# Two halves of the first expert product's columns: 512-column matrix products, an accumulating DMA, a gelu in a later job

## The chip, the cores and the metric

The program runs on one core of a Trainium2 chip. The metric is the time of one execution on the device, in microseconds (us); a lower time is better. The engines are TensorE (PE in the profile; PEld is its weight load), VectorE (DVE), ScalarE (ACT), GpSimd (POOL) and SyncE (SP). Each runs its own instructions in the order in which they stand, and waits for the others on semaphores. DMAs are issued from the queues of SP, ACT and, after the change, POOL.

## The reference, cut to what matters

Two encoder layers over 256 tokens of width 1024. Each has a token-mixing part and an expert part. The change works on the first product of the expert part. The reference looks 128 rows up per token in a table of 16384 rows:

```
act = jax.nn.gelu(jnp.einsum('cd,chkd->chk', hc, u_tab[ic]))
w = (gc * act.astype(jnp.float32)).astype(hc.dtype)
return jnp.einsum('chk,chkd->cd', w, v_tab[ic])
```

`hc` are tokens, `ic` the chosen rows (8 heads of 16), `gc` their weights by softmax.

## The kernel before, in words

The kernel doesn't gather rows. It multiplies all 256 tokens by all 16384 rows of `u_tab` (128 jobs of 128 rows), takes the gelu, multiplies by a table of weights that is zero where a row wasn't chosen, and multiplies the outcome by all of `v_tab` (128 more jobs). Both layers do so.

**Numbers in two parts.** TensorE works on float32r. To keep float32's precision each operand is split into a high and a low part: `hi` is the value rounded by an ACT copy (`split_hi`, L230), `lo` is what is left, by a DVE subtraction (`split_lo`, L233). A product is then three matmuls: low weights by high tokens (L238), high weights by low tokens (L239), high weights by high tokens (L240), which `prod` adds up in one PSUM tile. The weights are the 128x128 operand that is loaded, the tokens the one that streams: 256 columns. A job of the first expert product (`u_job`, L1031) has 8 chunks of the 1024 input features, so 24 matmuls.

**A job.** The loop at the end of the program takes each job of a list through the same steps: SP loads its 512 KB of weights (`raw`, three buffers), ACT writes `whi`, DVE writes `wlo` (three buffers each, two jobs ahead of use), TensorE multiplies into one of three PSUM banks (`main`), and the job's `post` empties the bank while the next job multiplies. In a first expert job `post` is a gelu on ACT, from PSUM. What it writes depends on how far the table of weights has got (`state["tok"]` tokens): with none it writes the gelu into the big table (L1050); else the tokens whose weights are there go to a tile `gel` (L1045) and DVE multiplies them into the table (L1048), and ACT writes the others (L1047).

**Work in the background.** While the 128 first expert jobs run, the choice of the rows is made in the background, in pieces of a fixed budget a job: on DVE the top 16 of scores and candidates (its recorded line is L93), then the table of weights, 64 blocks a layer, each with one-hot tiles on DVE (L970, L973), 8 small matmuls (`gw`, L988 and L989), DVE products (L998) and ACT copies (L1002).

**Order.** The program text is not the final order. A scheduling layer works out a time for each instruction and places it on its engine's queue by that; instructions recorded as in order (`VB`, `SB`) keep theirs. What stands on each queue must so be read from the built program.

**Storage.** Tiles come from pools; a tag names a place and `bufs` how many of it there are. `hhi` and `hlo` hold the tokens' high and low parts, `cst` the constants (identity, a row of numbers, cosines and sines of the rotary step), `gB1` a place that in turn holds `raws`, the gates `mixG`, and part of the table.

Of the kernel before, what the change touches and what calls it, by code (L numbers as in the profile page):

```python
# [22 lines left out]
NC8 = 8  # L23
# [5 lines left out]
LATE = 320 + DEPTH * 384  # L29
# [87 lines left out]
def _body(tc, nc, A, pp, big, hp, st, wk, ps, dr, stop, dump):  # L117
# [14 lines left out]
    cst = pp.tile([128, C_MASK], F32, name="cst")  # L132
    ident, iota = (cst[:, o:o + 128] for o in (C_ID, C_IOTA))
    cos, sin = cst[:, C_COS:C_COS + T], cst[:, C_SIN:C_SIN + T]
# [28 lines left out]
    def late_setup():  # L163
        nc.sync.dma_start(cst, A["cst"][:, :C_MASK])
        late = state["raws"][:, NAREA * D:]
        tmp = late[:, :320]
        nc.sync.dma_start(tmp, A["cst"][:, C_MASK:])
        for t, n in ((sink, "a_sink"),):
            nc.sync.dma_start(t, bass.AP(tensor=A[n].tensor, offset=A[n].offset, ap=[[0, 128], [1, 16]]))
# [11 lines left out]
        d2 = late[:, 320 + DEPTH * 256:].rearrange("p (a d) -> p a d", d=64)  # L181
# [53 lines left out]
    def prod(out, whi, wlo, xhi, xlo, n, start=True, stop=True):  # L235

        for c in range(n):
            PE.matmul(out, wlo(c), xhi(c), start=start and c == 0, stop=False)  # L238
            PE.matmul(out, whi(c), xlo(c), start=False, stop=False)  # L239
            PE.matmul(out, whi(c), xhi(c), start=False, stop=stop and c == n - 1)  # L240
# [46 lines left out]
    def new_h():  # L287
        hi = hp.tile([128, NC8, T], F32R, name="hhi", tag="hhi")
        lo = hp.tile([128, NC8, T], F32R, name="hlo", tag="hlo")
        return hi, lo  # L290

    def stats(r, m, direct):
# [7 lines left out]
        sq = wk.tile([128, T], F32, name="sq", tag="t1k", bufs=5)  # L300
# [53 lines left out]
    def norm_to_h(r, hi, lo, sc, sh, g, b):  # L354
# [10 lines left out]
        def emit(m):  # L365
            h = wk.tile([128, T], F32, name="hf", tag="t1k", bufs=5)
            S.activation(h, r[:, m], AF.Identity, scale=fold[:, 0, 0, m:m + 1], bias=fold[:, 0, 1, m:m + 1])
            marks["hi"] = split_hi(hi[:, m], h)
            marks["lo"] = split_lo(lo[:, m], h, hi[:, m])
# [17 lines left out]
    def start_chunk(m):  # L387
# [3 lines left out]
        hi, lo = state["h"]  # L391
        x = state["x"][:, m]
        V.tensor_scalar(opsc[:, m:m + 1], mods[0][:, 8 + m:9 + m], 1.0, None, op0=OP.add)
        h = wk.tile([128, T], F32, name="hf", tag="t1k", bufs=5)
        S.activation(h, x, AF.Identity, scale=opsc[:, m:m + 1], bias=mods[0][:, m:m + 1])
        split_hi(hi[:, m], h)
        split_lo(lo[:, m], h, hi[:, m])
# [20 lines left out]
    def layer(l):  # L418
# [3 lines left out]
        def mix_begin():  # L422
            m = big.tile([128, 64, T], F32, name="mixA", tag="gA")
            state["m"] = m
            state["bh"] = (big.tile([128, 24, T], F32R, name="mixB0", tag="gB0"), big.tile([128, 8, T], F32R, name="mixB2", tag="gB2"))
            mains((0, 1, 5))
            state["ab"] = []
            mf = m.rearrange("p a b -> p (a b)")
# [15 lines left out]
        def rope_post(n, slot, scale):  # L444
            def post(out):
                dst = state["m"][:, slot]
                rot = wk.tile([128, T], F32, name="ropet", tag="t1k", bufs=5)
# [4 lines left out]
                def gen(lane):  # L452
                    yield 0.0
                    V.tensor_tensor(dst, dst, cos, op=OP.mult)
# [10 lines left out]
        def v_post(dst):  # L465
            def post(out):
                raw = wk.tile([128, T], F32, name="vx", tag="t1k", bufs=5)
# [20 lines left out]
        def bchunk(a, k):  # L488

            k = 16 * a + k  # L490
            return state["bh"][0][:, k] if k < 24 else state["bh"][1][:, k - 24]

        def bsplit(src, k):
            split_hi(bchunk(0, k), src)
            split_lo(bchunk(1, k), src, bchunk(0, k))
# [84 lines left out]
        def head_c(lane, c):  # L580
# [25 lines left out]
            def tail(lane):  # L606
# [6 lines left out]
                sq = wk.tile([128, T], F32, name="sqc", tag="t1k", bufs=5)  # L613
# [105 lines left out]
        def gates_begin():  # L719
            state["gt"] = big.tile([128, 32, T], F32, name="mixG", tag="gB1")  # L720
        jobs.append(Job(func=gates_begin))
# [20 lines left out]
        def branch_job(m, half):  # L742
            def mm(hi, lo):
                out = main_bank([128, 2, T], name="main")
                for b in range(2):
                    o = 4 * (2 * half + b)
                    prod(out[:, b], lambda c: hi[:, 4 * b + c], lambda c: lo[:, 4 * b + c],
                         lambda c: bchunk(0, o + c), lambda c: bchunk(1, o + c), 4)
                return out

            def post(out):
# [4 lines left out]
                if half:  # L756
                    V.tensor_tensor(t, t, acc0, op=OP.add)
                    acc = wk.tile([128, T], F32, name="gacc", tag="t1k", bufs=5)
                    V.tensor_tensor(acc, t[:, 0], t[:, 1], op=OP.add)
                    xh, xl = state["mx"]  # L760
                    split_hi(xh[:, m], acc, scale=0.5)
                    V.scalar_tensor_tensor(xl[:, m], acc, 0.5, xh[:, m].bitcast(F32), op0=OP.mult, op1=OP.subtract)
# [26 lines left out]
        def out_job(m):  # L789
            def mm(hi, lo):  # L790
                out = main_bank([128, T], name="main")
                xh, xl = state["mx"]
                prod(out, lambda c: hi[:, c], lambda c: lo[:, c], lambda c: xh[:, c], lambda c: xl[:, c], NC8)
# [14 lines left out]
        def ln1():  # L808
            state["h"] = new_h()
            hi, lo = state["h"]  # L810
            norm_to_h(state["r"], hi, lo, mods[l][:, 32:40], mods[l][:, 24:32],
# [199 lines left out]
        def wq_job(k):  # L1011
            def mm(hi, lo):
                out = main_bank([128, T], name="main")
                xh, xl = state["h"]
                prod(out, lambda c: hi[:, c], lambda c: lo[:, c], lambda c: xh[:, c], lambda c: xl[:, c], NC8)
                return out

            def post(out):
                q = wk.tile([128, T], F32, name="qf", tag="t1k", bufs=5)
# [11 lines left out]
        def u_job(j):  # L1031
            def mm(hi, lo):
                out = main_bank([128, T], name="main")
                xh, xl = state["h"]
                prod(out, lambda c: hi[:, c], lambda c: lo[:, c], lambda c: xh[:, c], lambda c: xl[:, c], NC8)
# [306 lines left out]
```

## Time and profile before

| | |
|---|---|
| median of 3 runs | 2375.04 us (2373.57 to 2375.71) |
| the profiled execution's own time | 2374.35 us |
| span of its trace | 2372.5 us |
| TensorE busy | 2294.8 us, 97% of the span |
| VectorE busy | 1819.4 us, 77% |
| ScalarE busy | 1262.5 us, 53% |
| GpSimd busy | 0.2 us |

The span is the time from the first to the last instruction of the trace. Busy time is the time in which an engine has at least one instruction at work; matmuls overlap one another in it, so that it does not say how fast they follow each other. The starts of neighbouring rows of the timeline say that.

### The profile page before, as it was taken

To read this page: it belongs to the slowest core of one execution; us is meant where nothing else is said; L and a number is where in the kernel's file an instruction comes from. 1 tells how busy PE (TensorE), PEld (TensorE's weight loads), DVE (VectorE), ACT (ScalarE), POOL (GpSimd) and SP (SyncE) were. 2 spreads that over 40 slices of the span, in tenths; PEclk is the share of its full clock that TensorE was granted. 3 is DMA by queue.
4 is the path that set the end of the run, shared out by engine and by line. 5 is a ranking of instruction groups with operands and counts; after the bars stand their busy time and mean duration, and the time that the engine had idled before them with its cause. 6 is when DMAs were issued, how large, how long until landed. Compare 5 with 4: busy or idle time off the path is not lost.

```text
span 2372.5 us, 43573 instructions
## 1 busy us (share of the span) xinstructions
PE 2294.8 (97%) x16488; PEld 2129.3 (90%) x16488; DVE 1819.4 (77%) x3929; ACT 1262.5 (53%) x2539; POOL 0.2 (0%) x4
## 2 busy tenths in 40 slices
PE   6999999999999999999989999999999999999997
PEld 5999898999999988888789989999999999888886
DVE  8687788998889666667677867889888895665555
ACT  4755545455554454555467554455555544555444
POOL 0000000000000000000000000000000000000000
PEclk9999999999999999999989999999999999999998
DMA  8467654554545576767544765545544455665563
GB/s 335 155 228 255 213 188 146 169 183 160 163 159 163 181 229 238 248 237 254 193 155 154 260 226 202 189 149 172 178 161 161 161 169 195 238 209 194 194 212 107
DMA packets 128033, 461.80 MB, mean 195 GB/s; under 512 B 15440, under 2 KB 20048, under 8 KB 124624
## 3 DMA queue, kind: packets, MB, share of 16 engines
q1 hardware_dynamic: 126816, 453.25, 57.0%
q10 hardware_dynamic: 1008, 5.77, 0.6%
q8 instruction: 131, 2.15, 0.4%
q14 instruction: 78, 0.64, 0.1%
HBM read 450.31 MB, written 5.24 MB: 192 GB/s over the span
## 4 chain that ended last, share of the span: by engine, by line
PE 80%; DVE 13%; DMA 4%; ACT 2%; issue 2%; SPq 0%; DVEq 0%; ACTq 0%
PE main L238 15%; PE main L239 15%; PE main L240 15%; PE vacc L1077 10%; PE vacc L1076 10%; PE vacc L1078 10%; DVE wlo L233 4%; DMA mixA<-in_w_ada 2%; DVE topk L93 2%; PE gw L988 1%; PE gw L989 1%; DVE ada L252 1%; PE ssc L873 1%; ACT whi L230 1%; DMA raw<-in_w_out 1%
## 5 line engine op out<-in xcount | busy, mean ns | idle before, releaser
L233 DVE TENSOR_TENSOR wlo<-raw,whi 128x1024 fp32r<-128x1024 f32 x723 | 878.6, 1218 | 355.1 <-ACT whi L230 353.2
L238 PE MATMUL main<-hhi,wlo 128*128 128x256 f32 x3456 | 1002.1, 290 | 10.3 <-DVE wlo L233 9.5
L240 PE MATMUL main<-hhi,whi 128*128 128x256 f32 x3456 | 979.0, 283 | 0.0
L239 PE MATMUL main<-hlo,whi 128*128 128x256 f32 x3456 | 978.9, 283 | 0.0
L230 ACT ACTIVATE whi<-raw 128x1024 fp32r<-128x1024 f32 x720 | 761.7, 1058 | 393.5 <-PE vacc L1078 323.6
L238 PEld LDWEIGHTS main<-hhi,wlo 128*128 128x128 f32 x3456 | 663.3, 192 | 18.3 <-DVE wlo L233 12.1
L239 PEld LDWEIGHTS main<-hlo,whi 128*128 128x128 f32 x3456 | 664.3, 192 | 0.6
L240 PEld LDWEIGHTS main<-hhi,whi 128*128 128x128 f32 x3456 | 663.6, 192 | 0.0
L1077 PE MATMUL vacc<-wlo,wv 128*128 128x512 f32 x1024 | 398.6, 389 | 0.0
L1076 PE MATMUL vacc<-whi,wv 128*128 128x512 f32 x1024 | 398.6, 390 | 0.0
L1078 PE MATMUL vacc<-whi,wv 128*128 128x512 f32 x1024 | 398.4, 389 | 0.0
L1076 PEld LDWEIGHTS vacc<-whi,wv 128*128 128x128 f32 x1024 | 192.1, 188 | 40.3 <-ACT whi L230 0.4
L1077 PEld LDWEIGHTS vacc<-wlo,wv 128*128 128x128 f32 x1024 | 192.2, 188 | 40.0 <-DVE wlo L233 0.5
L1078 PEld LDWEIGHTS vacc<-whi,wv 128*128 128x128 f32 x1024 | 192.2, 188 | 39.8
L1045 ACT ACTIVATE gel<-main 128x256 f32<-128x256 f32 (+20 forms) x192 | 56.6, 295 | 298.7 <-PE main L240 298.7
L973 DVE TENSOR_TENSOR oha<-ohe,ijg 128x512 f16<-128x512 f16 x256 | 98.3, 418 | 0.9
L970 DVE TENSOR_TENSOR ohe<-iota,ijg 128x1024 f16<-128x1024 f16 x128 | 87.1, 682 | 0.2
L252 DVE CUSTOM_DVE_ANT_0 mixA<-mixA,cact,prm 128x1024 f32<-128x1024 f32 x48 | 61.5, 1280 | 32.0 <-DMA mixA<-in_w_ada 32.0
L1048 DVE TENSOR_TENSOR GB<-GB,gel 128x256 f32<-128x256 f32 (+29 forms) x128 | 46.6, 364 | 46.0 <-ACT gel L1045 44.5
L238 PE MATMUL main<-mixB,wlo 128*128 128x256 f32 x256 | 73.5, 290 | 2.2 <-ACT mixB L230 2.0
L239 PE MATMUL main<-mixB,whi 128*128 128x256 f32 x256 | 72.4, 284 | 0.0
L988 PE MATMUL gw<-ohe,oha 128*128 128x128 f16 x512 | 72.3, 222 | 0.0
(228 smaller groups left out, 2229.9 us busy)
## 6 DMA issues: line engine op xcount, KB each, us to landing
raw<-in_p_u SPq DMA_DIRECT2D x256, 512.0 KB, 3.3
raw<-in_p_v SPq DMA_DIRECT2D x256, 512.0 KB, 3.4
raw<-in_w_in SPq DMA_DIRECT2D x134, 512.0 KB, 4.2
mixA<-in_w_ada SPq DMA_DIRECT2D x48, 512.0 KB, 5.3
raw<-in_w_br SPq DMA_DIRECT2D x32, 512.0 KB, 3.3
adav<-in_w_ada SPq DMA_DIRECT2D x32, 512.0 KB, 4.5
raw<-in_p_wq SPq DMA_DIRECT2D x26, 512.0 KB, 3.5
ada<-in_w_ada SPq DMA_DIRECT2D x8, 1024.0 KB, 15.8
```

Source lines behind the costliest of these rows:

```text
L230: return S.activation(hi, src, AF.Copy, scale=scale)
L233: return V.tensor_tensor(lo, src, hi.bitcast(F32), op=OP.subtract)
L238: PE.matmul(out, wlo(c), xhi(c), start=start and c == 0, stop=False)
L239: PE.matmul(out, whi(c), xlo(c), start=False, stop=False)
L240: PE.matmul(out, whi(c), xhi(c), start=False, stop=stop and c == n - 1)
L252: V.tensor_tensor_reduce(out=buf[:, k], in0=buf[:, k], in1=state["cact"], scale=1.0, scalar=prm[:, P_BADA + 48 * l + n:P_BADA + 48 * l + n ...
L970: V.tensor_tensor(flat(eq), iota16.rearrange("p (c k) -> p c k", k=2)[:, None].to_broadcast([128, 2 * NB, 64, 2]), twice(ijg[:, 0:2]), op= ...
L973: V.tensor_tensor(flat(a[:, i:i + 1]), flat(eq[:, 0:1]), ijg[:, 2 + i, :, None, :].to_broadcast([128, NB, 64, 2]), op=OP.mult)
L988: PE.matmul(p[:, k], a[:, 0, k], b[:, k], start=True, stop=False)
L1076: PE.matmul(o, wl[:, tt], hi, start=first, stop=False)
L1077: PE.matmul(o, wh[:, tt], lo, start=False, stop=False)
L1078: PE.matmul(o, wh[:, tt], hi, start=False, stop=last)
```

## The change

- The tokens' two parts lie in one tile `h`, high and low side by side for each chunk.
- In the first expert product (`prod_apart`) the high weights meet both token parts in one matmul of 512 columns; the high part's sum lands in columns 0 to 255 of the bank and the low part's in 256 to 511. The low weights meet the high tokens in one of 256 columns, added to the first half. 16 matmuls a job instead of 24, with the same 768 columns a chunk.
- The halves must then be added. ACT copies both out of PSUM (`more`, `u`), and a DMA issued from POOL adds `more` to `u` (`accum_op`). The gelu (`gated`) works on `u`; the text calls it four jobs later, and the last four are called ahead of the second product.
- All other products still use three matmuls.
- To make room: cosines and sines no longer stay in `cst`, but are loaded into the gates' tile at each layer's start; the gates' tile is taken at the layer's start too; the row of numbers goes to a temporary place; the two `adav` tiles share the place of `h`.

```diff
+    def prod_apart(out, whi, wlo, x, n):
+
+
+        for c in range(n):
+            PE.matmul(out, whi(c), x(c), start=c == 0, stop=c == n - 1, skip_group_check=True)
+            PE.matmul(out[:, 0], wlo(c), x(c)[:, 0], start=False, stop=c == n - 1, skip_group_check=True)
...
     def new_h():
-        hi = hp.tile([128, NC8, T], F32R, name="hhi", tag="hhi")
-        lo = hp.tile([128, NC8, T], F32R, name="hlo", tag="hlo")
-        return hi, lo
+        return hp.tile([128, NC8, 2, T], F32R, name="h", tag="h")
...
             state["ab"] = []
+            state["gt"] = big.tile([128, 32, T], F32, name="mixG", tag="gB1")
...
+            nc.sync.dma_start(state["gt"][:, 6:8].rearrange("p a b -> p (a b)"), A["cst"][:, C_COS:C_COS + 2 * T])
...
         def u_job(j):
             def mm(hi, lo):
-                out = main_bank([128, T], name="main")
-                xh, xl = state["h"]
-                prod(out, lambda c: hi[:, c], lambda c: lo[:, c], lambda c: xh[:, c], lambda c: xl[:, c], NC8)
+                out = main_bank([128, 2, T], name="main")
+                x = state["h"]
+                prod_apart(out, lambda c: hi[:, c], lambda c: lo[:, c], lambda c: x[:, c], NC8)
                 return out
 
             def post(out):
                 while j >= 64 and state["GB0"] is None:
                     bgs["topk"].step(0)
+                u = wk.tile([128, T], F32, name="u", tag="t1k", bufs=6)
+                more = wk.tile([128, T], F32, name="more", tag="more", bufs=4)
+                S.activation(more, out[:, 1], AF.Copy)
+                S.activation(u, out[:, 0], AF.Copy)
+                nc.gpsimd.dma_start(u, more, accum_op=OP.add)
+                added.append(lambda: gated(u))
+                if len(added) > 4:
+                    added.popleft()()
+
+            def gated(u):
                 dst = slots(j, j + 1)[0][:, 0]
                 n = state["tok"]
                 if n:
-                    t = wk.tile([128, T], F32, name="gel", tag="t1k", bufs=5)
-                    S.activation(t[:, :n], out[:, :n], AF.Gelu_apprx_tanh)
+                    S.activation(u[:, :n], u[:, :n], AF.Gelu_apprx_tanh)
                     if n < T:
-                        S.activation(dst[:, n:], out[:, n:], AF.Gelu_apprx_tanh)
-                    V.tensor_tensor(dst[:, :n], dst[:, :n], t[:, :n], op=OP.mult)
+                        S.activation(dst[:, n:], u[:, n:], AF.Gelu_apprx_tanh)
+                    V.tensor_tensor(dst[:, :n], dst[:, :n], u[:, :n], op=OP.mult)
                 else:
-                    S.activation(dst, out, AF.Gelu_apprx_tanh)
+                    S.activation(dst, u, AF.Gelu_apprx_tanh)
                 state["jc"] = j + 1
             return Job(src=A["p_u"][l, j], mm=mm, post=post)
+        added = deque()
...
         def v_begin():
+            while added:
+                added.popleft()()
             drain()
```

TensorE's queue before, at the start of the first layer's first expert jobs (`main1` and `main5` are PSUM banks; the number behind a name tells one tile from another):

```order
L239 MATMUL main1_5092<-hlo_4290,whi_4984 128x256
L240 MATMUL main1_5092<-hhi_4289,whi_4984 128x256
...
L238 MATMUL main5_5134<-hhi_4289,wlo_5032 128x256
L239 MATMUL main5_5134<-hlo_4290,whi_5031 128x256
L240 MATMUL main5_5134<-hhi_4289,whi_5031 128x256
```

The same place after:

```order
L246 MATMUL main1_5091<-h_4289,whi_4983 128x512
L247 MATMUL main1_5091<-h_4289,wlo_4984 128x256
L246 MATMUL main5_5129<-h_4289,whi_5030 128x512
L247 MATMUL main5_5129<-h_4289,wlo_5031 128x256
L246 MATMUL main5_5129<-h_4289,whi_5030 128x512
```

Three matmuls of 256 columns a chunk have become one of 512 and one of 256.

ScalarE's queue before, in the same jobs (`GA` is the big table, `whi` the high weights of a job three further on):

```order
L1050 ACTIVATE GA_4393<-main1_5092 128x256
L230 ACTIVATE whi_5118<-raw_4998 128x1024
L1050 ACTIVATE GA_4393<-main5_5134 128x256
L230 ACTIVATE whi_5160<-raw_5045 128x1024
L1050 ACTIVATE GA_4393<-main0_5176 128x256
```

ScalarE's queue after, a few jobs on; between `L1048` of a tile `u` and `L1063` of the same number, POOL's DMA adds to that tile:

```order
L1047 ACTIVATE more_5516<-main0_5498 128x256
L1048 ACTIVATE u_5515<-main0_5498 128x256
L1063 ACTIVATE GA_4392<-u_5476 128x256
L230 ACTIVATE whi_5552<-raw_5457 128x1024
L1047 ACTIVATE more_5547<-main1_5529 128x256
L1048 ACTIVATE u_5546<-main1_5529 128x256
L1063 ACTIVATE GA_4392<-u_5515 128x256
L230 ACTIVATE whi_5591<-raw_5496 128x1024
L1047 ACTIVATE more_5586<-main5_5568 128x256
L1048 ACTIVATE u_5585<-main5_5568 128x256
L1063 ACTIVATE GA_4392<-u_5546 128x256
```

The gelu of a job (`u_5515`) stands behind the copies of the next job (`u_5546`), ahead of the next `whi`: one job later, not four. The scheduling layer has moved it up. The whole queue was read: the distance is one job for 248 of the 256 jobs, two or three for three jobs of each layer, none for each layer's last.

SyncE's queue before, at the start of the program:

```order
L1189 DMA raw_130<-in_w_in 128x1024
L164 DMA cst_82<-in_cst 128x768
L167 DMA raws_106<-in_cst 128x320
L169 DMA sink_80<-in_a_sink 128x16
L179 DMA raws_106<-in_c_lambda 128x512
L430 DMA mixA_241<-in_d_w 128x2048
L1189 DMA raw_277<-in_w_in 128x1024
```

The same place after:

```order
L1206 DMA raw_130<-in_w_in 128x1024
L162 DMA ident_82<-in_cst 128x128
L165 DMA raws_106<-in_cst 128x320
L167 DMA raws_106<-in_cst 128x128
L169 DMA sink_80<-in_a_sink 128x16
L179 DMA raws_106<-in_c_lambda 128x512
L436 DMA mixA_241<-in_d_w 128x2048
L441 DMA mixG_244<-in_cst 128x512
L1206 DMA raw_279<-in_w_in 128x1024
```

The load of cosines and sines into `mixG` stands ahead of the seventh job's weights (`raw_277`, now `raw_279`). It writes where `raws` was, so it waits for the last reader of `raws`.

## Rows read from the trace of the kernel before

**Rows 1.** The page's head: busy us, share of span, instructions.

```profile
span 2372.5 us, 43573 instructions
...
PE 2294.8 (97%) x16488; PEld 2129.3 (90%) x16488; DVE 1819.4 (77%) x3929; ACT 1262.5 (53%) x2539; POOL 0.2 (0%) x4
```

**Rows 2.** Timeline of PE: start us, duration us, instruction; first expert product.

```profile
599.84 0.28 PE L239 MATMUL main<-hlo,whi 128*128 128x256 f32 x1
...
601.04 0.28 PE L240 MATMUL main<-hhi,whi 128*128 128x256 f32 x1
```

**Rows 3.** Timeline of PE, second expert product.

```profile
899.70 0.39 PE L1076 MATMUL vacc<-whi,wv 128*128 128x512 f32 x1
...
902.88 0.39 PE L1078 MATMUL vacc<-whi,wv 128*128 128x512 f32 x1
```

**Rows 4.** Windows in the first expert product of layer one: busy us by engine.

```profile
core 0: us, PE busy (x) PEld busy (x) DVE busy (x) ACT busy (x) POOL busy (x), PEclk, DMA share, GB/s
440.00:460.00 20.00, 20.00 (x169) 20.00 (x168) 20.00 (x88) 9.38 (x14) 0.00 (x0) 1.00 0.54 182
460.00:480.00 20.00, 20.00 (x169) 20.00 (x168) 20.00 (x99) 9.41 (x14) 0.00 (x0) 1.00 0.53 173
500.00:520.00 20.00, 20.00 (x170) 20.00 (x169) 19.65 (x24) 9.17 (x15) 0.00 (x0) 1.00 0.52 165
760.00:780.00 20.00, 20.00 (x189) 19.79 (x188) 18.70 (x47) 9.63 (x25) 0.00 (x0) 1.00 0.52 165
```

**Rows 5.** Chain of waits from 440 to 520 us: shares by line.

```profile
by line: DVE topk L93 33.9%; DVE wlo L233 20.3%; PE main L238 14.9%; PE main L239 14.5%; PE main L240 14.4%; issue 1.8%; PE ijg L941 0.4%; DVEq L233 0.0%
```

**Rows 6.** Lines L1050 and L1045: count, ns min/median/max, first and last start, forms.

```profile
L1050 ACT ACTIVATE GA<-main x64: 384/384/387, 436.1 to 1694.1; 128x256 f32<-128x256 f32 x64
```

**Rows 7.** The same view of line L1045.

```profile
L1045 ACT ACTIVATE gel<-main x192: 173/298/384, 529.0 to 2003.1; 128x256 f32<-128x256 f32 x32, 128x4 f32<-128x4 f32 x4, 128x16 f32<-128x16 f32 x4, 128x24 f32<-128x24 f32 x4
```

**Rows 8.** Timeline of ACT, first expert jobs after the table of weights is done.

```profile
817.32 0.38 ACT L1045 ACTIVATE gel<-main 128x256 f32<-128x256 f32 x1 [1.55 <-PE main L240]
817.60 1.05 ACT L230 ACTIVATE whi<-raw 128x1024 fp32r<-128x1024 f32 x1
820.20 0.38 ACT L1045 ACTIVATE gel<-main 128x256 f32<-128x256 f32 x1 [1.55 <-PE main L240]
```

**Rows 9.** Timeline of ACT, jobs beside the table of weights.

```profile
640.91 0.26 ACT L1045 ACTIVATE gel<-main 128x108 f32<-128x108 f32 x1 [1.60 <-PE main L240]
641.07 0.29 ACT L1047 ACTIVATE GB<-main 128x148 f32<-128x148 f32 x1
641.24 1.06 ACT L230 ACTIVATE whi<-raw 128x1024 fp32r<-128x1024 f32 x1
642.20 0.49 ACT L1002 ACTIVATE GB<-gw 128x84 f32<-128x84 f32 x3
...
653.93 0.27 ACT L1045 ACTIVATE gel<-main 128x120 f32<-128x120 f32 x1 [1.99 <-PE main L240]
```

**Rows 10.** The page's DMA issues: count, KB each, median us from issue to landing.

```profile
raw<-in_p_u SPq DMA_DIRECT2D x256, 512.0 KB, 3.3
...
ropet<-mixA SPq DMA_DIRECT2D x104, 32.0 KB, 3.5
...
out_x<-r SPq DMA_DIRECT2D x8, 128.0 KB, 1.9
```

**Rows 11.** Line L450, the DMAs of `ropet` inside SBUF.

```profile
DMA to landing us min/median/max: 1.8/3.5/6.9
```

**Rows 12.** Timeline of the program's start: SyncE's queue, VectorE, ScalarE.

```profile
37.73 0.33 SPq L1189 DMA_DIRECT2D raw<-in_w_in  x1
...
42.87 0.41 DVE L184 TENSOR_REDUCE lams<-raws 128x4 f32<-128x256 f32 x1
...
45.47 1.05 ACT L230 ACTIVATE whi<-raw 128x1024 fp32r<-128x1024 f32 x1
```

More of the change, by code (lines that the diff above doesn't have):

```diff
@@ L167, in late_setup @@
         nc.sync.dma_start(tmp, A["cst"][:, C_MASK:])
+        iota = late[:, LATE - 128:]
+        nc.sync.dma_start(iota, A["cst"][:, C_IOTA:C_IOTA + 128])
         for t, n in ((sink, "a_sink"),):
@@ L233, in split_lo, with prod @@
         return V.tensor_tensor(lo, src, hi.bitcast(F32), op=OP.subtract)
-    def prod(out, whi, wlo, xhi, xlo, n, start=True, stop=True):
+    def prod(out, whi, wlo, x, n):
         for c in range(n):
-            PE.matmul(out, wlo(c), xhi(c), start=start and c == 0, stop=False)
-            PE.matmul(out, whi(c), xlo(c), start=False, stop=False)
-            PE.matmul(out, whi(c), xhi(c), start=False, stop=stop and c == n - 1)
+            PE.matmul(out, wlo(c), x(c)[:, 0], start=c == 0, stop=False)
+            PE.matmul(out, whi(c), x(c)[:, 1], start=False, stop=False)
+            PE.matmul(out, whi(c), x(c)[:, 0], start=False, stop=c == n - 1)
+    def prod_apart(out, whi, wlo, x, n):
+        for c in range(n):
+            PE.matmul(out, whi(c), x(c), start=c == 0, stop=c == n - 1, skip_group_check=True)
+            PE.matmul(out[:, 0], wlo(c), x(c)[:, 0], start=False, stop=c == n - 1, skip_group_check=True)
     def ada_load(l, i, buf, k=None):
@@ L438, in mm @@
                 state["out"] = out
[L439 to L440 removed]
+                x = state["h"]
+                prod(out, lambda c: hi[:, c], lambda c: lo[:, c], lambda c: x[:, c], NC8)
                 return out
@@ L486, in vtok, with bpair @@
             return state["m"][:, slot:slot + n].rearrange("p a b -> p (a b)").rearrange("p (t e) -> p t e", t=2)
-        def bchunk(a, k):
-            k = 16 * a + k
-            return state["bh"][0][:, k] if k < 24 else state["bh"][1][:, k - 24]
+        def bpair(k):
+            return state["bh"][0][:, k] if k < 12 else state["bh"][1][:, k - 12]
         def bsplit(src, k):
-            split_hi(bchunk(0, k), src)
-            split_lo(bchunk(1, k), src, bchunk(0, k))
+            p = bpair(k)
+            split_hi(p[:, 0], src)
+            split_lo(p[:, 1], src, p[:, 0])
         def to_keys(e, lane):
@@ L791, in mm @@
                 out = main_bank([128, T], name="main")
-                xh, xl = state["mx"]
-                prod(out, lambda c: hi[:, c], lambda c: lo[:, c], lambda c: xh[:, c], lambda c: xl[:, c], NC8)
+                x = state["mx"]
+                prod(out, lambda c: hi[:, c], lambda c: lo[:, c], lambda c: x[:, c], NC8)
                 return out
@@ L1123, in vstage @@
         def vstage(i, k):
-            if k == 0:
-                state["ada", i % 2] = hp.tile([128, 2, D], F32, name="adav", tag=("hhi", "hlo")[i % 2])
+            if i == k == 0:
+                both = hp.tile([128, 2, 2, D], F32, name="adav", tag="h")
+                for n in range(2):
+                    state["ada", n] = both[:, n]
             ada_load(*todo[i], state["ada", i % 2], k)
```

66 lines of the change are left out of this document (29 added, 37 removed).

## The prediction

> **What bounds the kernel now.** I read the page's head first [rows 1]: TensorE is busy in 97% of the span, VectorE in 77%, ScalarE in 53%, GpSimd not at all. Busy overlaps, so the second view is the timeline of TensorE, where the distance of starts is what counts. In the first expert product ten distances of 256-column matmuls take 601.04 - 599.84 = 1.20 us: 120 ns each [rows 2]. In the second, fourteen distances of 512-column matmuls take 902.88 - 899.70 = 3.18 us: 227.1 ns each [rows 3]. The second is not twice the first: 256 more columns cost 107.1 ns, so a matmul has some 12.9 ns of its own besides its columns (120 - 107.1). A first expert job has 24 matmuls, 2.88 us, and the timeline of ScalarE shows jobs exactly that far apart: 820.20 - 817.32 [rows 8]. Beside the table of weights four jobs take 653.93 - 640.91 = 13.02 us, 3.255 each [rows 9], since small matmuls of that table are added. So TensorE sets the pace of these jobs, at the granted clock 1.00 [rows 4].
>
> The third view is by windows, to see who comes next: VectorE is busy in all of 440 to 480 us, in 98% of 500 to 520, and in 94% at 760 to 780 [rows 4]. In the chain of waits of 440 to 520 us VectorE holds 54% (33.9 + 20.3) and TensorE's three lines the rest [rows 5]. There both are at their limit. That stage is 80 us long, some 80 / 2.88 = 28 jobs a layer.
>
> How many jobs are of which kind: 64 take the gelu with no weights there (L1050) [rows 6]; of 192 with weights 32 have all 256 columns, so come after the table is done [rows 7]. So 64 + 32 = 96 plain jobs, and 160 beside the table, in both layers.
>
> **The change part by part.**
>
> TensorE: a chunk of 120 x 3 = 360 ns becomes 227.1 + 120 = 347.1 ns. That is 12.9 ns a chunk, 103 ns a job (8 chunks), 26.4 us in 256 jobs. The columns are the same, so only the cost per matmul is saved. A plain job would go from 2.88 to 2.777 us, one beside the table from 3.255 to 3.152. Here a rule speaks for less. The Trainium skill (TensorE: Matmul & The Clock Gate, "Back-to-back issue gap") gives an isolated matmul about 2.5 ns besides its columns; 8 matmuls fewer in 256 jobs would then be worth 5 us. The rows show five times that in this stream of changing weights.
>
> VectorE: its work stays. In the 28 jobs a layer where it is full, a shorter TensorE job only waits for `wlo` sooner: I take their gain out, 56 x 0.103 = 5.8 us. Elsewhere it has 6% or more to spare, TensorE gains 3%.
>
> PSUM: the bank of a job is filled wholly instead of by half; there are three banks still, so nothing.
>
> ScalarE: per job it gets two copies of 256 columns from PSUM. The row nearest is the gelu from PSUM: 0.38 us, the next instruction starting 0.28 after it (817.60 - 817.32) [rows 8]. 0.56 us more a job on an engine that is busy for 9.6 of 20 us [rows 4], 1.6 of each 3.2 us: it fits. What it waits for is the matter. The gelu now waits for POOL's DMA, and the built order has it one job behind, not four. Behind that gelu stand in ScalarE's queue `whi` of a job to come, then the copies of the job after. So each DMA lies on a ring: `u` of job j copied, DMA j (its time from there to the waiting gelu I call L), gelu j, `whi`, copies of job j+2, DMA j+2. One turn of it is two jobs. In plain jobs the turn takes L + 0.28 (gelu) + 0.96 (`whi`, 642.20 - 641.24 [rows 9]) + 0.28 (`more`) + 0.38 (`u` to its end) = L + 1.90. Beside the table the gelu is 0.33 (641.24 - 640.91) and the copies out of `gw` 0.49 [rows 9]: L + 2.44. TensorE's two jobs take 5.554 and 6.304. The ring is hidden while L is under 3.65 us in plain jobs and under 3.86 beside the table; `whi` and `wlo` are made two jobs ahead, which covers the shift. If that cover is gone, a job takes half a turn. All jobs together then cost 96 x ((L + 1.90)/2 - 2.88) + 160 x ((L + 2.44)/2 - 3.255) = 128 L - 511 us against before: zero at L = 3.99, and 12.8 us for each tenth more.
>
> What L is, no row shows: POOL issues nothing before. From below: a DMA of the same 128 KB on SP's queue lands 1.9 us after its issue at the quiet end of the program [rows 10]. From above: 32 KB inside SBUF lands after 1.8 to 6.9 us, median 3.5, four of them in a row and behind weight loads [rows 10, 11]. At the place itself a weight load of four times the bytes lands after 3.3 us [rows 10], with the DMA engines busy 0.48 to 0.54 [rows 4]. The bytes are those of the first row, the place that of the last. I take 3.0, with the software queue and the second read in it, which would hide it. At 1.9 nothing changes; at 6.9 the formula gives +372 us. The Trainium skill (DMA: Bandwidth & Descriptors, "Anatomy of one DMA — SWDGE (gpsimd) path") gives about 2.0 us plus the bytes at 436 GB/s for one DMA from GpSimd; estimated from that page 2.3 us, which is hidden too. No run here shows a DMA of that queue.
>
> POOL's queue holds nothing else; a DMA that waits there holds only later ones of its kind, and `more` has four buffers. The 128 KB a job add a quarter to the bytes of a weight load, so a DMA share of 0.5 becomes some 0.63, and the weight loads' 3.3 us have three buffers.
>
> End of each layer's jobs: the last gelu waits for its own DMA, with the `whi` of the second product's third job ahead of it and the fourth behind. That one is needed three jobs later; nothing is lost. Without that cover it would cost L once a layer, 6 us.
>
> Program start: the seventh job's weights were issued at 37.73 us; now cosines and sines stand ahead and wait for the last reader of `raws`, which starts at 42.87 and takes 0.41 [rows 12]. The load goes out some 6 us later, at about 43.7, and lands some 4 us on, about 48. ScalarE wanted it at 45.47 [rows 12] and waits 2 to 3 us, within the two jobs of lead. I charge 0.5 us, at most 3. In layer two the same load stands behind weights and waits for nothing late. The merged `h` and `adav`, and the smaller constants, change places only.
>
> Sum: 26.4 - 5.8 - 0.5 = 20 us less than the profiled execution's 2374.35, so 2354. The runs' median is 0.7 us above that execution. 4.7 us (0.2%) is about what a measurement can tell from no change.
>
> **The rivals.**
>
> The ring decides (slower). Place: the gelu on ScalarE waiting for POOL's DMA in every job. It speaks for it that the built order leaves one job of lead, and that transfers in a busy queue have taken 3.5 us at the median and up to 6.9 [rows 10, 11]; against it the 1.9 us of an equal transfer. From L = 3.99 on it costs; at 4.22 it is +29 us, 2404 with the start's half us, at 4.5 +65, at 5.0 +129. Chance 0.28.
>
> A special form of it: GpSimd can't write its DMA's descriptors while VectorE works, so L grows by up to one `wlo`, 1.2 us, to 4.2: 128 x 4.2 - 511 = +27, 2401. Its chance, 0.05, is inside the 0.28. The Trainium skill (SBUF — State Buffer, "Who interferes with whom") has such a lock, for VectorE's two-port modes; by it two-tensor operations such as `wlo` don't take the lock for writing. Most of VectorE's work here is of that kind.
>
> Nothing changes (within 0.2%): the own cost of a matmul belongs to the change of weights and columns in another way than two rows of unmixed widths show, so a mixed pair takes near 360 ns; or L sits at 3.95 to 4.03. Then 2370 to 2380. Chance 0.10.
>
> VectorE binds longer: if the jobs at 94% are bound as well, another 50 jobs lose their 0.103 us, 5 us: 2359. Or not at all, and the 5.8 us come back: 2348. Both are still the forecast's case, whose own range is 2346 to 2364. Chance of faster by over 0.2%: 0.62, a tenth of it from L between 3.65 and 3.95.
>
> **How the numbers follow.** Faster 0.62, same 0.10, slower 0.28. The likeliest case gives 2354. Low end: all of the 26.4 us and nothing lost would be 2348, and 4 us more for what mixing widths may give, 2344; under it 0.04. High end: of the ring's 0.28 I leave 0.15 out, above L = 4.22: 2404.
>
> **What would show it.** Right: starts of a 512-column and the next matmul 227 and 120 ns apart; plain jobs 2.78 us apart, those beside the table 3.15; TensorE's idle small; landing of `u` under 3.6 us after issue; VectorE full from 440 to 520 us. Wrong: ScalarE's idle in front of the gelu (L1058, L1063) ended by POOL's DMA and TensorE's idle in front of L246 ended by `whi` or `wlo`: the ring. If pairs stand 360 ns apart, the saving per matmul was wrong. If weight loads land much later than 3.3 us and `whi` waits for them, the added transfers cost what I took as free.

## The result and the profile after

The change makes the kernel slower: 2521.6 us median of 4 runs (2517.82 to 2526.15) against 2374.89 us of 4 runs of the kernel before (2373.57 to 2375.71), a ratio of 1.0622 with a 95% interval of 1.0605 to 1.0640. The forecast was 2354 us, its range ended at 2404. The profiled execution's span is 2520.4 us, 147.9 more than [rows 1].

The page of the kernel after: the head with each engine's busy time, the DMA queue of GpSimd (packets, MB, share of 16 engines' span), the chain that ended last by engine, the groups of the DMA and of one gelu, and two DMA issues with their median time to landing.

```profile
PE 2335.8 (93%) x14440; PEld 2026.4 (80%) x14440; DVE 1811.5 (72%) x3919; ACT 1414.6 (56%) x3071; POOL 220.6 (9%) x260
...
q0 software_dynamic: 36864, 33.57, 8.6%
...
PE 47%; issue 26%; DVE 9%; DMA 7%; POOL 7%; ACT 2%; SPq 0%; POOLq 0%; DVEq 0%; ACTq 0%
...
L1049 POOL DMA_DIRECT2D u<-more x256 | 220.4, 861 | 1933.4 <-ACT u L1048 832.6
...
L1058 ACT ACTIVATE u<-u 128x256 f32<-128x256 f32 (+20 forms) x200 | 66.7, 333 | 296.5 <-DMA u<-more 296.3
...
raw<-in_p_u SPq DMA_DIRECT2D x256, 512.0 KB, 4.2
...
u<-more POOLq DMA_DIRECT2D x256, 128.0 KB, 5.2
```

No engine has become the bound: TensorE fell from 97% [rows 1] to 93% of a longer span. What is new is idle time that a DMA ends, 296.3 us in front of the gelu at L1058, and a time to landing of 5.2 us for `u`. Weight loads, 3.3 us before [rows 10], take 4.2. The chain books 26% as "issue", waits for which it finds no releaser; the timelines say what was waited for.

The views that the forecast named for the ring (copies of a job, its DMA, its gelu, then `whi` and the copies of a later job) show it. First the timelines of ScalarE and GpSimd in plain jobs (start, duration, instruction, idle time before it and what ended it):

```profile
469.97 0.42 ACT L1063 ACTIVATE GA<-u 128x256 f32<-128x256 f32 x1 [5.07 <-DMA u<-more]
470.30 1.04 ACT L230 ACTIVATE whi<-raw 128x1024 fp32r<-128x1024 f32 x1
471.24 0.36 ACT L1047 ACTIVATE more<-main 128x256 f32<-128x256 f32 x1
471.51 0.37 ACT L1048 ACTIVATE u<-main 128x256 f32<-128x256 f32 x1
471.77 0.41 ACT L1063 ACTIVATE GA<-u 128x256 f32<-128x256 f32 x1
472.07 1.05 ACT L230 ACTIVATE whi<-raw 128x1024 fp32r<-128x1024 f32 x1
473.02 0.38 ACT L1047 ACTIVATE more<-main 128x256 f32<-128x256 f32 x1
473.29 0.39 ACT L1048 ACTIVATE u<-main 128x256 f32<-128x256 f32 x1
477.36 0.42 ACT L1063 ACTIVATE GA<-u 128x256 f32<-128x256 f32 x1 [3.68 <-DMA u<-more]
...
472.17 0.86 POOL L1049 DMA_DIRECT2D u<-more  x1 [6.12 <-ACT GA L1063]
473.97 0.86 POOL L1049 DMA_DIRECT2D u<-more  x1 [0.94 <-ACT u L1048]
```

Read one turn: the gelu starts at 469.97, `whi` and both copies follow without a gap, `u` is done at 471.51 + 0.37 = 471.88, GpSimd issues at 472.17, and the gelu that waits for this DMA starts at 477.36. So L = 477.36 - 471.88 = 5.48 us, the rest of the turn 1.91 (the forecast had 1.90), the turn 7.39, and a turn is two jobs: 3.70 us a job.

The whole stage says the same. The first rows are the first expert product of layer one in the kernel before, its first matmuls (first and last start) and the first of the second product; then the same of the kernel after:

```profile
L238 PE MATMUL main<-hhi,wlo x1024: 279/283/385, 431.0 to 834.0; 128*128 128x256 f32 x171
L1076 PE MATMUL vacc<-whi,wv x512: 387/389/478, 834.4 to 1183.1; 128*128 128x512 f32 x171
```

```profile
L246 PE MATMUL main<-h,whi x1022: 390/395/775, 429.6 to 899.9; 128*128 128x512 f32 x171
...
L1092 PE MATMUL vacc<-whi,wv x512: 387/389/794, 903.2 to 1257.5; 128*128 128x512 f32 x171
```

Before, the stage takes 834.4 - 431.0 = 403.4 us, 3.15 a job. After, 903.2 - 429.6 = 473.6, which is 3.70 a job: the half turn. That is 70.2 us more in layer one. The second product, too, goes from 348.7 us to 354.3 between its first and last start, 5.6 us. Counted in the same way, layer two has 71.0 and 5.2 us. Together 152 us; the spans differ by 148.

VectorE and TensorE now idle, and the DMA engines are busier. Before, TensorE was busy in all of the two windows that follow, VectorE for 51.30 and 56.05 us of 60, with a DMA share of 0.49 and 0.51. The same windows of after (PE, PEld, DVE, ACT, POOL busy, then the granted clock, DMA share, GB/s):

```profile
600.00:660.00 60.00, 55.15 (x370) 45.86 (x369) 41.25 (x83) 38.32 (x132) 13.50 (x16) 1.00 0.77 177
720.00:780.00 60.00, 54.07 (x348) 45.01 (x347) 44.52 (x95) 35.03 (x113) 13.76 (x16) 0.94 0.70 169
```

VectorE is at 69% and 74%. 16 DMAs in 60 us are 3.75 us a job here as well. In the second window the mean granted clock is 0.94, stretches at 2.4 GHz and some at 1.2 GHz, beside 1.00 in [rows 4]; TensorE had idled in it for 6 us.

### The profile page after: what moved, and what is told of

It is laid out like the page before. It is cut to its first block, busy times and chain, and to the rows that moved or that the text cites. A ratio compares the mean times of both kernels' runs of the same rounds, so it can differ in the third digit from the quotient of the medians.

```text
span 2520.4 us, 40768 instructions
## 1 busy us (share of the span) xinstructions
PE 2335.8 (93%) x14440; PEld 2026.4 (80%) x14440; DVE 1811.5 (72%) x3919; ACT 1414.6 (56%) x3071; POOL 220.6 (9%) x260
## 3 DMA queue, kind: packets, MB, share of 16 engines
q0 software_dynamic: 36864, 33.57, 8.6%
## 4 chain that ended last, share of the span: by engine, by line
PE 47%; issue 26%; DVE 9%; DMA 7%; POOL 7%; ACT 2%; SPq 0%; POOLq 0%; DVEq 0%; ACTq 0%
PE vacc L1093 9%; PE vacc L1092 9%; PE vacc L1094 9%; POOL u L1049 7%; PE main L238 6%; PE main L239 5%; PE main L240 5%; DMA u<-more 4%; DVE wlo L233 3%; DMA mixA<-in_w_ada 2%; ACT whi L230 1%; DVE ada L259 1%; DMA raw<-in_w_in 1%; PE main L246 1%; DMA raw<-in_w_out 1%
## 5 line engine op out<-in xcount | busy, mean ns | idle before, releaser
L246 PE MATMUL main<-h,whi 128*128 128x512 f32 x2048 | 759.5, 410 | 23.9 <-ACT u L1048 23.7
L247 PE MATMUL main<-h,wlo 128*128 128x256 f32 x2048 | 588.5, 287 | 10.7 <-DVE wlo L233 10.2
L246 PEld LDWEIGHTS main<-h,whi 128*128 128x128 f32 x2048 | 394.3, 193 | 117.9 <-ACT u L1048 33.7
L238 PE MATMUL main<-h,wlo 128*128 128x256 f32 x1408 | 410.1, 292 | 11.4 <-DVE wlo L233 11.3
L247 PEld LDWEIGHTS main<-h,wlo 128*128 128x128 f32 x2048 | 396.2, 193 | 29.8 <-DVE wlo L233 29.2
L239 PE MATMUL main<-h,whi 128*128 128x256 f32 x1408 | 397.9, 283 | 0.0
L240 PE MATMUL main<-h,whi 128*128 128x256 f32 x1408 | 397.8, 283 | 0.0
L1049 POOL DMA_DIRECT2D u<-more x256 | 220.4, 861 | 1933.4 <-ACT u L1048 832.6
L238 PEld LDWEIGHTS main<-h,wlo 128*128 128x128 f32 x1408 | 269.0, 191 | 19.7 <-DVE wlo L233 13.5
L239 PEld LDWEIGHTS main<-h,whi 128*128 128x128 f32 x1408 | 269.6, 192 | 0.6
L240 PEld LDWEIGHTS main<-h,whi 128*128 128x128 f32 x1408 | 269.4, 191 | 0.0
L1058 ACT ACTIVATE u<-u 128x256 f32<-128x256 f32 (+20 forms) x200 | 66.7, 333 | 296.5 <-DMA u<-more 296.3
L992 PE MATMUL gw<-ohe,oha 128*128 128x128 f16 x512 | 79.4, 226 | 60.2 <-DVE oha L977 50.6
L1061 DVE TENSOR_TENSOR GB<-GB,u 128x256 f32<-128x256 f32 (+26 forms) x128 | 47.2, 370 | 91.6 <-ACT u L1058 61.4
```

The source lines that it names most:

```text
L238: PE.matmul(out, wlo(c), x(c)[:, 0], start=c == 0, stop=False)
L239: PE.matmul(out, whi(c), x(c)[:, 1], start=False, stop=False)
L240: PE.matmul(out, whi(c), x(c)[:, 0], start=False, stop=c == n - 1)
L246: PE.matmul(out, whi(c), x(c), start=c == 0, stop=c == n - 1, skip_group_check=True)
L247: PE.matmul(out[:, 0], wlo(c), x(c)[:, 0], start=False, stop=c == n - 1, skip_group_check=True)
L992: PE.matmul(p[:, k], a[:, 0, k], b[:, k], start=True, stop=False)
```

## The experiments

**Theories.** *Ring*: the gelu's lead is one job, a turn takes two, and L is too long for it. *Load*: the two copies and the added 128 KB a job cost the time by themselves, and the wait is only where it shows. *Pair*: a 512-column and a 256-column matmul save nothing against three of 256. *Rest*: the moved storage and loads cost the time.

### The lead, the wait, the work and the rest, one at a time

**Four jobs of lead.** The copies and the gelu are recorded in order, so that the gelu stands four jobs behind, as the text says:

```diff
-                S.activation(more, out[:, 1], AF.Copy)
-                S.activation(u, out[:, 0], AF.Copy)
+                SB.activation(more, out[:, 1], AF.Copy)
+                SB.activation(u, out[:, 0], AF.Copy)
...
-                    S.activation(dst, u, AF.Gelu_apprx_tanh)
+                    SB.activation(dst, u, AF.Gelu_apprx_tanh)
```

> Only ScalarE's order changes: the two copies and the gelu are kept in the order in which the code names them, so that the gelu really stands four jobs behind its copies. Ring theory: one turn now takes five jobs, 5 x 2.78 = 13.9 us of TensorE in plain jobs; with a DMA time L of about 5.5 us (5.2 from issue to landing and 0.3 ahead of it) the turn needs 5.5 + 1.9 = 7.4 us, so it is hidden, and the time is that of the forecast's sum, 2354 us (2346 to 2366). Load rival (ScalarE's two copies and the added 128 KB a job cost the time, the wait is only where it shows): the same copies and bytes remain, so about 2500 us. Pair rival (the mixed pair of matmuls saves nothing): 2370 to 2385.

Measured: 2369.49 us, ratio to before 0.9971 (0.9958 to 0.9983). `u` still lands after 5.3 us at the median, yet 152 us are back: the price was the lead, not the transfer's work. 15 us are missing to 2354; the next runs part them.

**The work without the wait.** The gelu reads PSUM; copies and DMA follow it, and nobody waits for the sum.

```diff
+                    S.activation(dst, out[:, 0], AF.Gelu_apprx_tanh)
...
                 S.activation(more, out[:, 1], AF.Copy)
                 S.activation(u, out[:, 0], AF.Copy)
                 nc.gpsimd.dma_start(u, more, accum_op=OP.add)
-                added.append(lambda: gated(u))
```

> The gelu reads the first half straight from PSUM; both copies and the accumulating DMA are still issued, behind it, and nothing waits for the sum, so the term of the weights' high part and the tokens' low part is left out of the output. Ring theory: 2354 us or a few above it (2346 to 2368), though every added copy and byte is there. Load rival: about 2500 us, as the work is the same. The DMA's landing tells whether 5.2 us is a matter of the place: with jobs 2.78 us apart the transfers come more often, so it stays at 4.5 to 6 us by contention; if it falls under 3.5 us, the bunching that the ring makes was what slowed it.

Measured: 2367.92 us, ratio 0.9968 (0.9956 to 0.9981), the top of the ring's range. So the load is not the cause of the 147 us. The DMA lands after 5.0 us, so the bunching of the transfers in the ring didn't make it long.

**No adding at all.**

```diff
-                S.activation(more, out[:, 1], AF.Copy)
-                S.activation(u, out[:, 0], AF.Copy)
-                nc.gpsimd.dma_start(u, more, accum_op=OP.add)
-                added.append(lambda: gated(u))
+                    S.activation(dst, out[:, 0], AF.Gelu_apprx_tanh)
```

> The two products apart as in the change, the gelu straight from the first half in PSUM, no copies and no DMA; the term of the weights' high part and the tokens' low part is left out of the output. It is the floor of TensorE's part: 2374.9 - 26.4 + 5.8 + 0.5 = 2354 us by the forecast's terms (2346 to 2360). If it stays at 2370 or above, the saving of 12.9 ns a chunk does not reach the time, whatever the ring does.

Measured: 2361.51 us, ratio 0.9933 (0.9916 to 0.9950), so 12 to 20 us are saved, some 16 where the forecast had 20. With the two runs above, some 6 us are the work of copies and accumulating DMAs that nobody waits for. TensorE's timeline shows why a part of the saving is missing. The rows are a job's second and last 512-column matmul, six pairs apart, first of a job at 449 us, then of one beside the table:

```profile
449.37 0.39 PE L246 MATMUL main<-h,whi 128*128 128x512 f32 x1
...
451.45 0.39 PE L246 MATMUL main<-h,whi 128*128 128x512 f32 x1
...
701.51 0.40 PE L246 MATMUL main<-h,whi 128*128 128x512 f32 x1
...
703.63 0.40 PE L246 MATMUL main<-h,whi 128*128 128x512 f32 x1
```

In the first job six pairs take 2.08 us, 347 ns each, just what the forecast put together from two unmixed streams; in the second 2.12 us, 353 each, so 7 ns are saved there, not 12.9. Counted over both layers of this run, 115 of the 256 jobs stand at 347 and 137 at 353. What decides between the two levels, no run shows.

**The rest alone.** Only the first product goes back to three matmuls and a gelu from PSUM.

```diff
-                prod_apart(out, lambda c: hi[:, c], lambda c: lo[:, c], lambda c: x[:, c], NC8)
+                prod(out, lambda c: hi[:, c], lambda c: lo[:, c], lambda c: x[:, c], NC8)
```

> The first expert product is as before (three matmuls a chunk, the gelu from PSUM), and all else of the change stays: the joint storage of the two token parts, the cosines and sines loaded late, the smaller constants, six small buffers. By the forecast's terms it costs 0.5 us, so 2375 us, the same as before within 3 us. If these moves cost a part of the 147 us, it shows here: more than 2380.

Measured: 2375.23 us, ratio 1.0001 (0.9992 to 1.0011). Storage, constants and the late cosines cost nothing that this run can tell, so at most some 3 us. Of the 15 us that the run with four jobs misses, 7.5 are then TensorE's smaller saving (2361.51 against 2354), 6.4 the copies and DMAs, and 1.6 the wait, which is within the noise.

### The lead, swept

As in the run with four jobs, with `if len(added) > 2` and `> 1`.

> As the run with four jobs, but the gelu two jobs behind its copies. Ring theory: a turn takes three jobs, 3 x 2.78 = 8.3 us in plain jobs, against 5.5 + 1.9 = 7.4 us needed: hidden at the median landing of 5.2 us, and only landings over 6.1 us would show. So the time of the run with four jobs, 2369 us, to 10 us above it. Without a ring (a fixed cost of each wait on the queue) the distance would matter little and this run would lie near neither.

Measured: 2385.41 us, ratio 1.0038 (1.0022 to 1.0055), 16 us above four jobs and so above what was expected. Landings there are 5.4 us at the median and up to 7.9; the ring has room for 6.1, and the gelus still wait 71.9 us (59.0 and 12.9, by ScalarE's two groups of them) for the DMA, against 8.6 with four jobs.

> The gelu one job behind its copies, by the code's order instead of by the scheduling layer's. Ring theory: a turn is two jobs again, 7.4 us for 5.55, so the time of the change, 2522 us within 15. If ScalarE's order as the scheduling layer chose it had another fault than the distance, this run would be as fast as those with two or four jobs, about 2370.

Measured: 2591.59 us, ratio 1.0903 (1.0879 to 1.0927): a two-job ring again, but 70 us worse than the change, which was not expected. ScalarE beside the table in this run (L93 is the line of all that is recorded in order), and then in the change:

```profile
703.10 0.29 ACT L93 ACTIVATE u<-u 128x104 f32<-128x104 f32 x1 [0.15 <-DMA u<-more]
703.30 0.31 ACT L93 ACTIVATE GB<-u 128x152 f32<-128x152 f32 x1
705.35 0.51 ACT L1006 ACTIVATE GB<-gw 128x92 f32<-128x92 f32 x3 [1.74 <-DVE GB L1002]
705.73 0.40 ACT L93 ACTIVATE more<-main 128x256 f32<-128x256 f32 x1
```

```profile
703.24 0.37 ACT L1048 ACTIVATE u<-main 128x256 f32<-128x256 f32 x1
703.50 0.48 ACT L1006 ACTIVATE GB<-gw 128x72 f32<-128x72 f32 x3
705.45 0.32 ACT L1058 ACTIVATE u<-u 128x140 f32<-128x140 f32 x1 [1.46 <-DMA u<-more]
```

In the change the scheduling layer often put the table's copies (L1006) ahead of the waiting gelu, where they lie in the DMA's shadow. In the code's order they stand behind it, inside the turn, and with them a wait for VectorE's product. With the forecast's L + 2.44 beside the table instead of L + 1.90, 160 jobs would each take half the difference, 0.27 us, longer; by that estimate it is 43 of the 70 us. The mean granted clock is lower as well, 0.86 at 720 to 780 us against 0.94; how much of the other 27 us that is, no run parted.

### What makes L long

**A plain copy** in the place of the accumulating DMA, in the order of the change:

```diff
-                nc.gpsimd.dma_start(u, more, accum_op=OP.add)
+                nc.gpsimd.dma_start(u, more)
```

> The order of the change, the gelu one job behind, but GpSimd's DMA is a plain copy of the second half over the first, so the output lacks the first half. It tells whether the accumulation makes the transfer long. With half a turn, (L + 1.9)/2, for each of 256 jobs, as the trace of the change has it, the time is 2375 + 128 L - 564: every tenth of a us less in L gives 12.8 us back, down to some 2369 us below L = 4.4. Accumulation theory: the landing falls from 5.2 to 3.5 us or less (the 3.3 us of a weight load of before), and the time to about 2370. Place theory (queue, descriptors and the other transfers make it long, not the adding): landing 4.9 to 5.3 us and 2490 to 2525.

Measured: 2360.75 us, ratio 0.9940 (0.9923 to 0.9956). The page of this run, GpSimd's queue and issues:

```profile
q0 software_dynamic: 12288, 33.57, 4.0%
...
raw<-in_p_u SPq DMA_DIRECT2D x256, 512.0 KB, 3.7
...
u<-more POOLq DMA_DIRECT2D x256, 128.0 KB, 2.2
```

Same queue, same bytes, same gelu one job behind: 2.2 us instead of 5.2, and 161 us less. The same bytes go in 12288 packets instead of 36864, and in 4.0% of the DMA engines' span instead of 8.6%. The time is also that of the run with no adding at all, so both copies and a plain 128 KB a job are hidden.

**In quiet.** Seven DMAs behind the last output, each waiting for the one before; the third to fifth of them:

```diff
+                nc.gpsimd.dma_start(pb, pa, accum_op=OP.add)
+                nc.scalar.dma_start(pc, pb)
+                nc.gpsimd.dma_start(pc, pb, accum_op=OP.add)
```

> The run with four jobs and, behind the last output, a chain of seven DMAs of 128 KB inside SBUF, each waiting for the one before: plain and accumulating from GpSimd, plain from SyncE and from ScalarE. It measures the disputed price with no other transfer near. Chosen in the forecast was 3.0 us for L. If the plain one of GpSimd lands after 2 to 2.5 us and the accumulating one after 2.5 to 3, the price in the stage is made by the weight loads beside it (2.5 us of the 5.2). If the accumulating one takes 4.5 us or more in quiet too, it is the operation's own.

The DMA issues of this run (the first of the next rows, with a count of 2, is the median of a plain and an accumulating one):

```profile
quietb<-quieta POOLq DMA_DIRECT2D x2, 128.0 KB, 2.3
quietc<-quietb ACTq DMA_DIRECT2D x1, 128.0 KB, 2.0
quietc<-quietb POOLq DMA_DIRECT2D x1, 128.0 KB, 2.7
quietd<-quietc SPq DMA_DIRECT2D x1, 128.0 KB, 2.0
quietd<-quietc POOLq DMA_DIRECT2D x1, 128.0 KB, 2.0
```

Plain 2.0 us from each of the three queues, accumulating 2.7, each row but the first one single DMA. So neither the operation in quiet (2.7) nor the place for a plain copy (2.2) gives 5.2: it takes both together. The run's time, 2387.31 us, has the seven DMAs in it.

**Smaller packets, no adding.** `dma_start(u[:, :T - 1], more[:, :T - 1])`, 255 columns.

> As the run with the plain copy, but of 255 instead of 256 columns, so that a row of a partition is its own packet, as in the accumulating DMA (the first half's first 255 columns are overwritten, so the output lacks them). It parts the adding from the cutting into small packets. Theory of the adding: landing stays near the plain copy's 2.2 us, the time near 2361 us. Theory of the packets (128 of about 1 KB in place of 32 of 4 KB make the transfer long): landing 3.5 us or more, and by 2375 + 128 L - 564 with L = landing + 0.3 at 5.2 again some 2515 us.

Measured: 2360.38 us, ratio 0.9942 (0.9924 to 0.9959), landing 2.3 us. But GpSimd's queue again shows 12288 packets, so the rows were not cut apart: the run leaves open whether small packets or the adding make the transfer long.

**Half the bytes, adding.** `dma_start(u[:64], more[:64], accum_op=OP.add)`.

> The order of the change, with the accumulating DMA over 64 of the 128 partitions (the other half of the first half's term is left out). It tells what in the accumulating transfer takes the 3 us more than a plain one in the stage. If it is the work on the data (packets of 1 KB, added one by one), half of them take half: landing some 3.7 us, L = 4.0, hidden, 2360 to 2375 us. If it is a fixed price of an accumulating DMA in a busy place, the landing stays at 4.8 to 5.2 and the time at 2475 to 2525.

Measured: 2459.35 us, ratio 1.0360 (1.0332 to 1.0387). Landing:

```profile
q0 software_dynamic: 20480, 16.79, 5.3%
...
u<-more POOLq DMA_DIRECT2D x256, 64.0 KB, 4.5
```

Half the bytes take 0.7 us off the median. On that line 128 KB would carry at most 1.4 of the 3.0 us between an accumulating and a plain DMA, and 1.6 don't go with the bytes. But the landings spread (2.5 to 6.5 us), and the means over 256 of them say otherwise: 5.04 us in the change, 4.11 here, 2.72 for the plain copy, so that up to 1.9 of 2.3 us would go with the bytes. The run shows that the amount counts, and leaves open how much of the price is fixed. With L = 4.5 + 0.3 = 4.8 a half turn of (L + 1.90)/2 in all 256 jobs, against two stages of 403.4 before, gives 2375 + 128 x 4.8 - 564 = 2425, and the run is 34 us above. A reason may be that the median hides the spread: beside the table a landing over 4.1 us (6.304 - 1.90 - 0.3) costs, and one under it returns nothing. That is argued, not shown.

### Other ways to add

**GpSimd adds in SBUF**, the gelu one job behind: `nc.gpsimd.tensor_tensor(u, u, more, op=OP.add)`.

> No DMA: GpSimd itself adds the two copies in SBUF, the gelu one job behind in the code's order. Ring theory: GpSimd's addition stands in the ring in the DMA's place; if it takes under 3 us, it is hidden at one job's distance too, and the time is the plain copy's 2361 us or a little less, complete this time. Rival: GpSimd and VectorE get in each other's way in SBUF, where VectorE is full (440 to 520 us of each layer), then 2365 to 2385.

Measured: 2416.55 us, ratio 1.0181 (1.0161 to 1.0200), slower than either expectation. The group of the addition, then VectorE's multiplication of the gelu into the table of weights in this run and in the run with four jobs:

```profile
L1049 POOL TENSOR_TENSOR u<-u,more 128x256 f32<-128x256 f32 x256 | 295.4, 1155 | 1751.1 <-ACT u L93 1710.3
...
L1061 DVE TENSOR_TENSOR GB<-GB,u 128x256 f32<-128x256 f32 (+28 forms) x128 | 85.5, 668 | 5.9 <-ACT u L93 5.7
L1061 DVE TENSOR_TENSOR GA<-GA,u 128x4 f32<-128x4 f32 (+25 forms) x66 | 41.2, 624 | 10.7 <-ACT u L93 10.7
```

```profile
L1061 DVE TENSOR_TENSOR GB<-GB,u 128x256 f32<-128x256 f32 (+26 forms) x128 | 46.7, 368 | 9.4 <-ACT u L93 9.4
L1061 DVE TENSOR_TENSOR GA<-GA,u 128x4 f32<-128x4 f32 (+17 forms) x72 | 15.3, 212 | 9.3 <-ACT u L93 9.3
```

The addition takes 1.16 us at the mean, and VectorE is busy for 1909.2 us, 99 more than in the run with four jobs, with nearly the same instructions (3927 and 3919). The multiplications shown took 65 us longer in all, `wlo` 20 (878.4 to 898.9); both read two tiles in SBUF. The Trainium skill (SBUF — State Buffer, "Who interferes with whom") states that a VectorE instruction with two SBUF inputs contends with a GpSimd instruction that reads SBUF; the rows agree. The instructions that choose the rows (L93) took some 30 us longer too, but nearly as much in the next run, where GpSimd adds nothing, so they don't speak for the contention. That VectorE's longer work is what cost the 42 us is likely, not shown: VectorE is busy for 59.66 of 60 us at 720 to 780, and TensorE for 56.91.

**VectorE adds**, from PSUM, with one copy only: `V.tensor_tensor(u, out[:, 0], more, op=OP.add)`.

> No DMA and one copy only: VectorE adds the first half, from PSUM, to the copied second. No ring of any length is left; VectorE gets about 0.4 us a job more. Where it has 6% or more to spare that is hidden, in the 28 jobs a layer where it is full it costs 0.4 us each, 22 us, and in jobs at 94% some of it: 2375 to 2395 us. It tells whether VectorE is the bound there, as the forecast said when it took 5.8 us off.

Measured: 2378.13 us, ratio 1.0012 (1.0003 to 1.0022). Windows:

```profile
440.00:480.00 40.00, 36.59 (x201) 30.43 (x200) 39.42 (x172) 22.33 (x39) 0.00 (x0) 1.00 0.48 143
480.00:520.00 40.00, 37.95 (x212) 32.04 (x211) 39.61 (x114) 25.24 (x43) 0.00 (x0) 1.00 0.61 178
...
720.00:780.00 60.00, 60.00 (x413) 51.00 (x412) 59.18 (x147) 34.98 (x95) 0.00 (x0) 1.00 0.52 158
```

In layer one TensorE loses 5.5 us from 440 to 520 us and nothing from there to the stage's end, though VectorE has 99% at 720 to 780. So with this addition VectorE is the bound where the forecast put it, and the jobs at 94% are not. The run without adding says how much of the forecast's 5.8 us that is: the first 16 jobs of a layer gain 0.115 us each there, though VectorE is full, and the next 16 nothing (2.96 and 3.04 us a job in the two layers against 2.96 before).

**Mixed.** The first 32 jobs of a layer as before, the other 96 with VectorE's addition.

> A version meant to beat both, drawn from the runs before: the first 32 jobs of a layer, where VectorE is full, as in the kernel before (three matmuls a chunk, the gelu from PSUM), the other 96 with the products apart, one copy and VectorE's addition, no DMA. If the 12 us between the run with VectorE's addition and the run without any addition (2378 minus 2361, less the clock) come from the stage where VectorE is full, they are gone here: 192 jobs save 8 x some 10 ns each, 15 us, so 2360 us (2356 to 2366). If VectorE's addition costs beside the table too, 2366 to 2376.

Measured: 2369.16 us, ratio 0.9974 (0.9964 to 0.9984). TensorE is full from 560 us on and loses 1.8 us where the two kinds meet (520 to 560); the hoped 2360 isn't reached. This and the run with four jobs are complete versions that beat both kernels, the one before by 0.3%.

## Why the prediction was wrong

**The step that failed is the price of L**: "I take 3.0, with the software queue and the second read in it, which would hide it". L measured 5.48 in the turn shown: 5.2 to landing and 0.3 ahead of the issue. The two rows it was taken from speak of plain copies, and for a plain copy they were right: 2.2 us in the stage (run with the plain copy), near the 1.9 of [rows 10]. The accumulation was charged as a detail ("the second read"); in this place it is 3.0 us. The page that the forecast cites (the Trainium skill, DMA: Bandwidth & Descriptors, "Anatomy of one DMA — SWDGE (gpsimd) path") gave 2.3 us: the plain copy agrees, the accumulating one does not.

**The ring was right**, and on record as the rival with 0.28: the rest of the turn 1.91 (1.90 forecast), two jobs a turn, 3.70 us a job. Its formula gives 128 x 5.48 - 511 = +190, the stages lost 140. Most of the difference, 43 us, is the L + 2.44 beside the table, where the copies of the table lay in the DMA's shadow; the rest is that the stages before took 2 x 403.4 = 807 us and not the 797 of the forecast's jobs. With 1.90 for all 256 jobs the stages take 256 x (5.48 + 1.90) / 2 = 945 us: +138. The range ended at 2404, since it left out the part of the ring above L = 4.22; a slope of 12.8 us for each tenth over a price between 1.9 and 6.9 called for a wider one.

**TensorE's saving was right in kind, somewhat too large**: 12 to 20 us in the run without adding instead of 20; 347 ns a pair as forecast in 115 of 256 jobs, 353 in 137.

**VectorE** full up to 520 us: right, but about half of those jobs gained all the same (run without adding). **Start**: half a us charged, too little for any run to show (run of the rest). **Copies on ScalarE**: hidden, right (plain copy). **The added bytes**: hidden for a plain copy, not for the accumulating one. With four jobs the run is 2369.49 us, 9 above the plain copy, and weights land after 4.5 us (3.3 before). **End of a layer**: costed at nothing because of a cover, and at 6 us a layer without it; the second product took 5.6 us longer. At 900 to 930 us, where the last gelus of the ring hold `whi` back, TensorE is busy for 25.59 of 30 us at a mean granted clock of 0.94; from 930 on it is full.

**GpSimd held up by VectorE while it writes descriptors**: refuted. In the change its issue takes 0.86 us, min/median/max 859/859/1004 ns, and 0.86 in quiet too; and the plain copy, issued in the same place, lands after 2.2 us.

## What to carry to other kernels

A lead written in code counts only as it stands in the built order: take from there how many jobs one turn of a ring has, and compare the latency plus the rest of the turn with that many jobs' time. A latency that no row shows is priced by its operation too, not by its bytes alone; where the sum has a slope on it, the range must hold both bounds, and one run with the operation swapped (here a plain copy for an accumulating one) told more than any estimate. Before an addition goes to another engine, see whom it meets there: a DMA, GpSimd and VectorE each had a price of its own here.

## What was not expected of the hardware

An accumulating DMA of 128 KB inside SBUF landed after 2.7 us in quiet and 5.0 to 5.4 beside weight loads, a plain one after 2.0 and 2.2. It took three times the packets (36864 against 12288) and 0.86 instead of 0.54 us to issue, and the weight loads beside it landed later (4.5 us, 3.7 beside plain copies and also with no added DMA). What part of the price is the adding and what the small packets stays open. GpSimd's addition of 128x256 took 1.16 us, and VectorE's instructions with two inputs in SBUF took some 85 us longer beside 256 of them.
